# A row-wise gradient of an 8192 x 8192 matrix: the stores move from SyncE's DMA queue to ScalarE's

## The chip, the cores and the metric

The kernel runs on one core of one Trainium2 chip. A core has five engines with instruction streams of their own (TensorE, VectorE = DVE, ScalarE = ACT, GpSimd = POOL, SyncE = SP) and 16 DMA engines that move data between the chip's memory (HBM) and the core's on-chip memory (SBUF, 128 partitions). A DMA is issued by an instruction on one of the engines' streams; the instruction waits in that stream for its semaphores, and what it issues then joins that engine's DMA queue. The metric is the device time of one execution in microseconds (us), given as the median of several.

## The reference

The input is one float32 matrix, and the reference is one call:

```python
def setup_inputs():
    return {
        "x": np.random.randn(8192, 8192).astype(np.float32),
    }

def reference(x: np.ndarray) -> np.ndarray:
    return np.gradient(x, axis=1)
```

Along each row, every inner element becomes half the difference of its two neighbours, (x[j+1] - x[j-1]) / 2. The first element becomes x[1] - x[0], the last one x[8191] - x[8190]. Rows are independent. The kernel has to read 268.44 MB and to write 268.44 MB.

## The kernel before

The 8192 rows are cut into 32 sets of 256 rows. In a set, each of the 128 partitions holds two whole rows, 16384 numbers or 64 KB, side by side. A set is loaded with one DMA and stored with one DMA, each of 128 pieces of 64 KB (8.39 MB in all), so 8 pieces for each of the 16 DMA engines. The sets are grouped by three (`NB = 3`): in a group a partition's six rows are consecutive in memory, and set k of the group takes rows 2k and 2k+1 of the six. The last group has two sets.

There are three slots in SBUF, one for each set of a group, and set i lives in slot i % 3. A slot has 64 elements more than a set. The load puts the data behind that space (at `SH = 64`), and the result is written from the slot's beginning, so that the output overwrites input that has already been read. One slot therefore serves load, computation and store of a set in turn.

For each set, five steps follow each other:

- L55, the load, issued on SP's queue. A load of set i from 3 on needs the slot free, which is when the store of set i - 3 has landed.
- L65, POOL: the differences at the two ends of each row go into the small tile `ends` (128x4), before the computation overwrites them.
- L71, DVE: one custom instruction over the whole slot takes the differences of neighbours two apart and halves them (128x16382).
- L82, POOL for some sets and DVE for the others: the four end values are put in their places in the result.
- L84, the store of the set, which needs L82.

The order is written out by hand. SP's stream holds both kinds of DMA: the loads of sets 0, 1 and 2, then the stores of sets 0, 1 and 2, then the loads of sets 3, 4 and 5, then their stores, and so on to the end. The loop that produces this issues the store of set i on SP in each turn, and after the last set of a group it issues the loads of the whole next group. An instruction of SP's stream that waits holds up everything behind it in that stream. The helper `chain` declares which steps an instruction has to wait for: the load for the store of its slot, the first step for the load, and so on down to the store.

Of the kernel before, what the change touches and what calls it, by code (L numbers as in the profile page):

```python
# [1 line left out]

# [4 lines left out]


@with_exitstack
def kernel(  # L10
    ctx: ExitStack,
    tc: tile.TileContext,
    x: bass.AP,
    out: bass.AP,
):
    nc = tc.nc
    P = nc.NUM_PARTITIONS
    n, m = x.shape
    R = 2
    NB = 3  # L20
    SH = 64
    W = R * m
    nsets = n // (P * R)
    f32 = x.dtype

    def sets(a):
        found = []
        for first in range(0, nsets, NB):
            q = min(NB, nsets - first)
            rows = a[first * P * R : (first + q) * P * R, :].rearrange("(p q) m -> p (q m)", p=P)  # L30
            found += [rows[:, k * W : (k + 1) * W] for k in range(q)]
        return found

    x_sets, out_sets = sets(x), sets(out)

    pool = ctx.enter_context(tc.tile_pool(name="pool", bufs=1))
    pad = pool.tile([P, 32], f32, name="pad", tag="pad")
    slots = [pool.tile([P, SH + W], f32, name=f"slot{k}", tag=f"slot{k}") for k in range(NB)]
    ends = pool.tile([P, nsets, R, 2], f32, name="ends", tag="ends")
    loads, stores = [], [None] * nsets  # L40
    in_front = {}

    def chain(i, ins, *needed):
        group, engine = f"slot{i % NB}", ins.ins.engine
        keep = [o.ins for o in needed]
        if in_front.get(engine, (None,))[0] == group:
            keep.append(in_front[engine][1])
        tc.declare_no_dep(ins.ins, group=group, keep=keep, reason="implied by the needed step")
        tc.add_to_no_dep_group(group, ins.ins)
        in_front[engine] = group, ins.ins  # L50
        return ins

    def load(i):
        b = slots[i % NB]
        ins = nc.sync.dma_start(out=b[:, SH : SH + W], in_=x_sets[i])  # L55
        loads.append(chain(i, ins, *([stores[i - NB]] if i >= NB else [])))

    with tc.manual_schedule():
        for i in range(NB):
            load(i)  # L60
        for i in range(nsets):
            b = slots[i % NB]
            xin = b[:, SH : SH + W].rearrange("p (t m) -> p t m", m=m)

            ins = nc.gpsimd.tensor_sub(  # L65
                out=ends[:, i, :, :],
                in0=xin[:, :, 1 : m : m - 2],
                in1=xin[:, :, 0 : m - 1 : m - 2],
            )
            at = [chain(i, ins, loads[i])]  # L70
            ins = nc.vector._custom_dve(  # L71
                dve_ops.TENSOR_TENSOR_REDUCE_SUB_MAX,
                out=b[:, 1 : W - 1],
                in0=b[:, SH + 2 : SH + W],
                in1=b[:, SH : SH + W - 2],
                s0=0.0,
                s1=0.5,
            )
            halved = chain(i, ins, *at)
            res = b[:, 0:W].rearrange("p (t m) -> p t m", m=m)  # L80
            placer = nc.gpsimd if i % 5 in (1, 3) and i < nsets - 2 else nc.vector
            ins = placer.tensor_copy(out=res[:, :, 0 : m : m - 1], in_=ends[:, i, :, :])  # L82
            placed = chain(i, ins, halved)
            ins = nc.sync.dma_start(out=out_sets[i], in_=b[:, 0:W])  # L84
            stores[i] = chain(i, ins, placed)
            if i % NB == NB - 1:
                for k in range(i + 1, min(i + 1 + NB, nsets)):
                    load(k)


# [1 line left out]
_INS = ['x']  # L92
_OUTS = [((8192, 8192), 'float32')]


# [23 lines left out]
```

## Time and profile before

| | us |
|---|---|
| Median of 3 runs (1245.47 to 1245.9) | 1245.82 |
| Profiled execution | 1246.23 |
| Its span in the profile | 1244.3 |
| DVE busy, 52 instructions | 554.6 |
| of which L71, 32 instructions of 17.224 us | 551.2 |
| POOL busy, 48 instructions | 8.9 |
| Load, median from issue to landing | 57.9 |
| Store, median from issue to landing | 40.4 |

The profile is of one execution. Its span is a little shorter than the time measured for that execution. "Busy" counts the work of an engine's instructions; issuing a DMA and waiting for semaphores are not counted. The page cuts the span into 40 equal slices of 31.1 us, and gives for each the busy share of the engines and of the 16 DMA engines, with what they moved in GB/s. A row of the timeline gives the start, the duration, the engine (SPq is the instruction stream of SP as an issuer of DMAs), the line, the tiles and, in brackets, the idle time before it and what ended it. Several instructions of one kind in a row are drawn together as x3, and the duration is then from the first to the last of them. A row of the waits gives the total, the count and the longest. A row of the table by stretches gives the stretch, its length, the busy time of DVE and of POOL with counts, the granted clock, the DMA engines' busy share and GB/s. Beside these views the trace holds a record of each DMA packet, with its start, its duration and its size.

### The profile page before, as it was taken

To read this page: it belongs to the slowest core of one execution; us is meant where nothing else is said; L and a number is where in the kernel's file an instruction comes from. 1 tells how busy PE (TensorE), PEld (TensorE's weight loads), DVE (VectorE), ACT (ScalarE), POOL (GpSimd) and SP (SyncE) were. 2 spreads that over 40 slices of the span, in tenths; PEclk is the share of its full clock that TensorE was granted. 3 is DMA by queue.
4 is the path that set the end of the run, shared out by engine and by line. 5 is a ranking of instruction groups with operands and counts; after the bars stand their busy time and mean duration, and the time that the engine had idled before them with its cause. 6 is when DMAs were issued, how large, how long until landed. Compare 5 with 4: busy or idle time off the path is not lost.

```text
span 1244.3 us, 237 instructions
## 1 busy us (share of the span) xinstructions
DVE 554.6 (45%) x52; POOL 8.9 (1%) x48
## 2 busy tenths in 40 slices
DVE  2850583069009603850582079009603840591082
POOL 0000000000000000000000000000000000000000
DMA  9999999999999999999999999999999999999999
GB/s 404 438 436 423 421 438 438 438 438 436 434 423 430 434 438 438 430 436 432 428 434 436 432 436 434 438 436 430 432 428 438 436 434 438 434 434 430 430 409 404
DMA packets 9217, 536.88 MB, mean 431 GB/s; under 512 B 1024, under 2 KB 1024, under 8 KB 1024
## 3 DMA queue, kind: packets, MB, share of 16 engines
q1 hardware_dynamic: 9216, 536.88, 99.8%
q14 instruction: 1, 0.01, 0.0%
HBM read 268.44 MB, written 268.44 MB: 431 GB/s over the span
## 4 chain that ended last, share of the span: by engine, by line
another core or an unknown queue 74%; DVE 18%; DMA 3%; issue 2%; POOL 1%; SPq 0%; POOLq 0%
DVE slot L71 18%; DMA slot<-in_x_dram 3%; POOL ends L65 0%; POOL slot L82 0%; SPq L55 0%; POOLq L114 0%; DVE slot L82 0%
## 5 line engine op out<-in xcount | busy, mean ns | idle before, releaser
L71 DVE CUSTOM_DVE_ANT_0 slot<-slot 128x16382 f32<-128x16382 f32 x32 | 551.2, 17224 | 667.2 <-POOL ends L65 667.2
L65 POOL TENSOR_TENSOR ends<-slot 128x4 f32<-128x4 f32 x32 | 6.4, 200 | 988.1 <-DMA slot<-in_x_dram 988.1
L82 POOL COPY slot<-ends 128x4 f32<-128x4 f32 x12 | 2.3, 192 | 207.9 <-DVE slot L71 207.9
L82 DVE COPY slot<-ends 128x4 f32<-128x4 f32 x20 | 3.4, 172 | 0.7
L103 POOL MEMSET const-bfloat16-1.0<- 128x1 bf16 x1 | 0.1, 102 | 0.0
L103 POOL MEMSET const-uint8-127<- 128x1 uint8 x1 | 0.1, 102 | 0.0
L103 POOL MEMSET const-float32-0.0<- 128x1 f32 x1 | 0.1, 99 | 0.2 <-issue 0.2
L103 POOL MEMSET const-float32-1.0<- 128x1 f32 x1 | 0.1, 99 | 0.0
## 6 DMA issues: line engine op xcount, KB each, us to landing
slot<-in_x_dram SPq DMA_DIRECT2D x32, 57.9
out_dram<-slot SPq DMA_DIRECT2D x32, 40.4
```

What stands on the lines that cost most here:

```text
L65: ins = nc.gpsimd.tensor_sub(out=ends[:, i, :, :], in0=xin[:, :, 1 : m : m - 2], in1=xin[:, :, 0 : m - 1 : m - 2],)
L71: ins = nc.vector._custom_dve(dve_ops.TENSOR_TENSOR_REDUCE_SUB_MAX, out=b[:, 1 : W - 1], in0=b[:, SH + 2 : SH + W], in1=b[:, SH : SH + W - 2],
L82: ins = placer.tensor_copy(out=res[:, :, 0 : m : m - 1], in_=ends[:, i, :, :])
L103: nc = _bacc.Bacc("TRN2", target_bir_lowering=False, num_devices=1)
```

## The change

The store of each set is issued on ACT's stream and queue instead of SP's. SP's stream then holds the 32 loads alone, in the same order, and ACT's the 32 stores, in the same order; ACT has no other work. The load of set i from 3 on still waits for the store of set i - 3, and a store for the placed ends, but neither stands behind instructions of the other kind. Nothing changes on POOL or DVE.

```diff
@@ -81,7 +81,7 @@
             placer = nc.gpsimd if i % 5 in (1, 3) and i < nsets - 2 else nc.vector
             ins = placer.tensor_copy(out=res[:, :, 0 : m : m - 1], in_=ends[:, i, :, :])
             placed = chain(i, ins, halved)
-            ins = nc.sync.dma_start(out=out_sets[i], in_=b[:, 0:W])
+            ins = nc.scalar.dma_start(out=out_sets[i], in_=b[:, 0:W])
             stores[i] = chain(i, ins, placed)
             if i % NB == NB - 1:
                 for k in range(i + 1, min(i + 1 + NB, nsets)):
```

## The prediction

> **What bounds the kernel now.** I read the page from its top first: the span, the engines' rows, the slices, the queue's share.
>
> ```profile
> span 1244.3 us, 237 instructions
> ...
> DVE 554.6 (45%) x52; POOL 8.9 (1%) x48
> ...
> DMA  9999999999999999999999999999999999999999
> ...
> q1 hardware_dynamic: 9216, 536.88, 99.8%
> ```
>
> No engine is near the bound: DVE works 45% of the span. The 16 DMA engines are busy in all 40 slices, and the single queue q1 accounts for 99.8% of their time. What the transfers cost is the whole time.
>
> Next, how fast they run in each direction. The table by stretches takes stretches of 58 us, as long as a batch of three transfers:
>
> ```profile
> 2.00:60.00 58.00, 34.62 (x3) 0.59 (x3) 1.00 0.99 420
> 60.00:118.00 58.00, 17.39 (x2) 0.20 (x1) 1.00 1.00 434
> 118.00:176.00 58.00, 33.98 (x2) 0.59 (x3) 1.00 1.00 434
> 176.00:234.00 58.00, 18.03 (x4) 0.20 (x1) 1.00 1.00 434
> ```
>
> The last number is GB/s. The first and third rows are loads almost alone, the second and fourth stores almost alone: 434 GB/s both ways. The packet records behind these views say the same: a 64 KB packet takes 2.418 us in nearly every record and its engine starts the next one 2.415 us later, load or store. A transfer has 8 packets an engine, so 19.32 us. 64 transfers make 512 packets an engine: 512 x 2.415 = 1236.5 us of the 1244.3.
>
> Third, the order. The timeline at the start, and the waits of SP's queue:
>
> ```profile
> 0.74 1.33 SPq L55 DMA_DIRECT2D slot<-in_x_dram  x3
> ...
> 40.46 39.91 SPq L84 DMA_DIRECT2D out_dram<-slot  x3
> ...
> 81.69 39.18 SPq L55 DMA_DIRECT2D slot<-in_x_dram  x3
> ```
>
> ```profile
> SPq L84 <- DVE slot L82: 525.5, 20, 55.9
> SPq L55 <- DMA out_dram<-slot: 372.9, 29, 19.1
> SPq L84 <- POOL slot L82: 299.0, 12, 36.7
> ```
>
> SP stands waiting nearly always, and it costs nothing, because the transfers it has issued stand one behind the other: three loads, three stores, three loads. Store 0 is issued at 40.46 but its first packet starts at 61.4, behind loads 1 and 2. Load 3 is issued at 81.69, just after store 0 has landed, while stores 1 and 2 still have 38 us to run.
>
> Fourth, what is left over, from the packet records (means over 16 engines). 1.9 us to the first packet; 0.72 us extra on that packet; 1.02 us extra on the last load packet ahead of store 0, the first crossing from loading to storing; 0.95 us together on the last load packet at the nine later such crossings (0.19, 0.02, 0.12, 0.30, 0.12, 0.13, 0.03, 0.00, 0.04: mean 0.105); nothing of note at the ten crossings from stores to loads (0.02 at most); 1.7 us of empty DMA engines near the end, where store 30 is issued late; 1.4 us after the last packets. With 1236.5 that is 1244.2, the span. The end itself:
>
> ```profile
> 1203.28 19.61 SPq L84 DMA_DIRECT2D out_dram<-slot  x2
> 1204.86 0.20 POOL L65 TENSOR_TENSOR ends<-slot 128x4 f32<-128x4 f32 x1 [19.07 <-DMA slot<-in_x_dram]
> 1205.09 17.22 DVE L71 CUSTOM_DVE_ANT_0 slot<-slot 128x16382 f32<-128x16382 f32 x1 [1.84 <-POOL ends L65]
> 1222.35 0.17 DVE L82 COPY slot<-ends 128x4 f32<-128x4 f32 x1
> ```
>
> Load 31 ends, DVE takes 17.2 us, store 31 is issued about 1222.6 and its packets start at 1223.5; store 30 covers all but 1.7 us of that.
>
> **The change part by part.** The profiled execution took 1246.23 us, 1.93 beyond its span, and the median shown is 1245.82, 0.41 less. So I make the span's sum and add 1.5.
>
> *The issues themselves.* 32 store issues of about 0.34 us each (the row of L84) leave SP's queue and stand on ACT's. ACT has no work: the page has no row for it. An issue there waits, as before, for the placed ends (L82). Its semaphore waits on older transfers name ones that have landed before. Cost nothing: one issue against 38 us between stores, covered by whatever transfer is running. If that cover were gone, 32 x 0.34 = 11 us.
>
> *The wait that goes.* Load i+3 stood behind the issues of the whole batch of stores; now it waits only for store i. In the timeline what it ended on was the landing of store 0 anyway, and at that moment 38 us of stores were queued. Taking the wait away is worth 0 by itself: the DMA engines had no gap there to fill.
>
> *The wait that comes.* Stores no longer stand behind loads 1 and 2. Store 0's packets begin at about 40.5 + 0.9 = 41.4 us (0.9 is the time from issue to first packet of stores 30 and 31), while load 2's have just begun. From there two queues offer work to the same 16 engines. If they share evenly, a transfer takes 2 x 19.32 = 38.6 us instead of 19.3. Does a slot then starve the engines? A slot's round is load 38.6, about 18 of POOL and DVE (0.2 + 17.2 + 0.2 and the gaps), store 38.6, about 3 for issues and landings: 98 us. Three slots bring six transfers of work, 116 us. So 18 us are to spare: when a store lands, the next one has been ready for about 18 us. After each store's landing the load queue is empty for 1 to 3 us; the store queue has it all then, so the engines stay busy. Cost 0. It would turn into idle only if POOL and DVE took over 36 us a set.
>
> *The tail.* Loads and stores end in step, so load 31 is out when store 30 has most or all of its 8 packets left. Store 31 can start 21.0 us after load 31's mean end (1202.5 to 1223.5 in the rows), store 30 covers 19.3: the same 1.7 us gap, or 4.1 if one packet of store 30 (2.4 us) has already gone. I take 1.7.
>
> *The crossings.* This is the new work. Before, an engine crossed from loading to storing 11 times and back 10 times. Now the engine alternates. Load 2's 8 packets and the 232 of loads 3 to 31 each stand between store packets: about 240 crossings from load to store, and as many back. No stretch of this trace has both directions queued at once, so the price is bounded. Lower end: 0, by the crossings from store to load; below zero is a rival. Upper end: the first crossing, 1.02 us, x 240 = 245 us. It stands alone: the nine later crossings average 0.105 and the largest is 0.30. The slowest engine gives a nearer upper end: from the load issue at 81.69 to that at 1127.60 lie nine rounds of 116.21 us, 0.29 over 48 x 2.415 = 115.92. I take 0.105, the mean over engines of the steady crossings, since what is alternated is just such steady packets: 240 x 0.105 = 25.2 us. At 0.29 it is 69.6 us. The 1.97 us of old crossings go into this count.
>
> Sum: 1.9 + 0.7 + 1236.5 + 25.2 + 1.7 + 1.4 = 1267.4 us of span; with 1.5, **1269 us**.
>
> The Trainium skill (DMA: Bandwidth & Descriptors, Rules for kernel authors) states that spreading DMAs over SP, ACT and GpSimd does not raise bandwidth, as all run on the same 16 engines and interleave; by that the sum would stay without the 25.2 us, the first rival below. The same page (Latency and other measured facts) gives 214 GB/s in each direction as the full rate of copies on the two queues; as an estimate from that page, 536.88 MB at 428 GB/s is 1254 us, and with the ends 1261. No row here has both directions in flight, so the trace does not decide between them.
>
> **The rivals.**
>
> *Sharing is free.* The engines alternate at 2.415 us a packet. For it: the same rate in both directions and free crossings from store to load. Against: nine of ten times something was lost from load to store. 1.9 + 0.7 + 1236.5 + 1.7 + 1.4 + 1.5 = 1243.7 us, or 1246 with the longer tail.
>
> *The two directions overlap (the other side: faster).* One place: inside a DMA engine a load packet and a store packet run partly at once, from 41 us to 1202 us. Both kinds run at 434 GB/s alone, which fits a limit on each direction as well as a limit on the sum. A pair now takes 4.83 us; each 0.1 us less over 240 pairs is 24 us, so 1220. It decides from 0.002 us a pair on, since the free case lies just above the bound. Against: if the engine could take in the next packet's data while it puts out the last, the crossings from load to store should have been shortened, and they were lengthened.
>
> *Every crossing costs like the first, or in that direction.* Above 0.29 us each: beyond 1313 us, at 1.02 us 1489. For it: the first crossing is the only one into a fresh stream, and a second queue is one too. Against: nine later ones.
>
> **How the numbers follow.** About 0.2% (2.5 us) is what a measurement of this kernel can tell from no change: 1243.3 to 1248.3. Crossings at 0.02 to 0.29 us (1248.3 to 1313): 0.60. Free sharing: 0.20. Overlap: 0.11. Dear crossings: 0.09. Slower is 0.60 + 0.09 = 0.69, same 0.20, faster 0.11. The range from 1243 to 1314 leaves out the overlap and the dear crossings, 0.20.
>
> **What would show it.** Two queues in the page's third part, about half of the packets each. Loads and stores of 38 us to landing each, rather than 57.9 and 40.4. GB/s in the stretches from 60 us on: 425 by the forecast (434 x 4.83 / 4.94), 434 if sharing is free, above it if directions overlap. DVE's groups at 17.2 us and every store ready well ahead of its first packet; if the DMA row shows less than 9 in the middle, a slot starves and the 18 us were counted wrong. The packet records should be longer around alternations; if packets stand at 2.418 us and the time still grows, it is gaps between them. The prediction is wrong if the price of alternating isn't that of a crossing in one queue, which is its weakest step.

## The result, and the profile after

The changed kernel takes 1251.39 us in the median of five runs (1250.07 to 1255.29) against 1245.82 (1245.18 to 1245.94): a ratio of 1.0049, 95% interval 1.0034 to 1.0064. It is slower, as forecast, but by 5.6 us and not by 23. The runs also spread over 5 us, where those of the kernel before stay within 0.8. The profiled run, 1250.07 us, is the fastest of the five. Ratios, here and below, leave out the three runs that took over 1.5% more than the fastest of their kernel; the ranges hold them.

The page of the changed kernel, its span, DMA rows and queues:

```profile
span 1247.8 us, 264 instructions
...
DMA  9999999999999999999999999999999999999997
GB/s 403 437 437 437 437 424 426 429 435 435 437 437 437 437 437 437 435 426 424 429 437 435 435 437 435 437 437 437 437 429 426 433 431 437 433 437 437 437 437 311
...
q1 hardware_dynamic: 4608, 268.44, 49.8%
q10 hardware_dynamic: 4608, 268.44, 49.6%
```

The two queues halve the packets. The engines are full in every slice but the last: 311 GB/s there, where the kernel before had 404. The stretches, in the columns used before (length, DVE, POOL, clock, DMA share, GB/s):

```profile
60.00:118.00 58.00, 17.39 (x2) 0.20 (x1) 1.00 1.00 434
600.00:658.00 58.00, 24.32 (x3) 0.39 (x2) 1.00 1.00 434
1000.00:1058.00 58.00, 20.80 (x2) 0.59 (x3) 1.00 1.00 434
1208.00:1227.00 19.00, 17.39 (x2) 0.20 (x1) 1.00 0.65 283
1227.00:1247.00 20.00, 0.00 (x0) 0.00 (x0) 1.00 0.97 419
```

With loads and stores sharing the engines the rate is 434 GB/s, the very number of pure loading and pure storing. The loss is in the fourth row: for 19 us the engines are 65% busy. The timeline of that place:

```profile
1208.62 0.20 POOL L65 TENSOR_TENSOR ends<-slot 128x4 f32<-128x4 f32 x1 [38.31 <-DMA slot<-in_x_dram]
1208.85 17.22 DVE L71 CUSTOM_DVE_ANT_0 slot<-slot 128x16382 f32<-128x16382 f32 x1 [21.07 <-POOL ends L65]
1226.11 0.17 DVE L82 COPY slot<-ends 128x4 f32<-128x4 f32 x1
```

POOL sees load 31 at 1208.62 (1204.86 before). DVE works until 1226.3, store 31 follows, and the engines have run out of store 30 by then: 6.1 us of empty engines in the mean, by the packet records, against 1.7 before.

The packet records show how the queues share: from store 0's first packet on, wherever both queues have work, an engine takes one whole 64 KB packet of the one and then one of the other, each 2.418 us long. Between 100 and 1190 us 87% of the packets follow one of the other queue. The Trainium skill (DMA: Bandwidth & Descriptors, Queues, rings and completion order) states that an engine goes round-robin over its queues and switches at packet boundaries only; the records agree, packet by packet. The Trainium skill's rule that two issuing engines only interleave (same page, Rules for kernel authors) was the better of the two weighed ahead: 434 GB/s is above 428, the estimate from the 214 GB/s in each direction that the Trainium skill (same page, Latency and other measured facts) states for copies between HBM tensors.

For what follows, two quantities from the packet records. The *lateness* of an engine is how far its packets are behind 1.75 us + 2.415 us a packet; the slowest of the 16 counts, because a transfer has landed only when all have done their part. (The records don't name the engine. They are put in 16 chains by their times; in each chain every transfer has 8 packets and one record of 4 bytes behind them.) The *landing delay* is the time from the last packet of a load to POOL's start on it. In this trace the delay is 0.41 and 0.37 us for loads 0 and 1, which ran alone, and 2.82 to 3.17 from load 2 on, which shared: 2.4 us more, the length of one packet of the other queue. The 4-byte records say why. For loads 0 and 1 this record starts as soon as the engine's last packet has ended. On the engine that finishes last with load 31 it starts at 1208.21, one store packet (2.41 us) after the load's last packet, and POOL starts 0.41 us later; it is the same 2.41 us for every load from 2 on. What reports a landing waits its turn, too.

The first account of the 3.5 us between the profiled spans: load 31's last packet ends at 1205.8, where it was 1204.5 (+1.3: the slowest engine is 6.2 us late and no longer 4.9); POOL starts on it 2.82 us later and not 0.35 (+2.5); from POOL's start to the end it is 39.2 us and was 39.4 (-0.2).

### The profile page after: what moved, and what is told of

Same layout as the page of the kernel before. It is cut to its first block, busy times and chain, and to the rows that moved or that the text cites. A ratio compares the mean times of both kernels' runs of the same rounds, so it can differ in the third digit from the quotient of the medians.

```text
span 1247.8 us, 264 instructions
## 1 busy us (share of the span) xinstructions
DVE 554.6 (44%) x52; POOL 8.8 (1%) x48
## 4 chain that ended last, share of the span: by engine, by line
another core or an unknown queue 83%; DMA 9%; issue 3%; DVE 3%; SPq 1%; POOL 0%; POOLq 0%
DMA slot<-in_x_dram 5%; DMA out_dram<-slot 3%; DVE slot L71 3%; SPq L55 1%; POOL ends L65 0%; DVE slot L82 0%; POOLq L114 0%
```

## The experiments

**Is it the end or the sharing?** Four kernels. First, the last two stores back on SP's queue:

```diff
-            ins = nc.scalar.dma_start(out=out_sets[i], in_=b[:, 0:W])
+            storer = nc.sync if i >= nsets - 2 else nc.scalar
+            ins = storer.dma_start(out=out_sets[i], in_=b[:, 0:W])
```

> Stores 30 and 31 go back to SP's queue, where they stand behind load 31; stores 0 to 29 stay on ACT's. Theory 'tail' (alternating packets is free; the loss is the 6.1 us, mean over DMA engines, in which they stand empty ahead of store 31, because part of store 30 has already gone beside load 31): store 30 lies whole behind load 31 again, the gap is about 1.7 us as before the change, and the time is 1245 to 1247 us. Theory 'mixing' (sharing the engines costs a little all the way from 41 us on): the time stays at 1250 to 1252 us.

Measured: 1251.43 us (1248.03 to 1255.31), ratio 1.0044 (1.0028 to 1.0060). 'Tail' as I had put it missed; the time is that of 'mixing'. Second, only the last eight stores on ACT's queue:

```diff
-            ins = nc.scalar.dma_start(out=out_sets[i], in_=b[:, 0:W])
+            storer = nc.scalar if i >= nsets - 8 else nc.sync
+            ins = storer.dma_start(out=out_sets[i], in_=b[:, 0:W])
```

> Only stores 24 to 31 are issued on ACT's queue, stores 0 to 23 stay on SP's. 'Tail': the end is that of the changed kernel, so nearly the whole loss is there, 1249 to 1252 us, with 4 to 7 us of empty engines ahead of store 31. 'Mixing': the two directions share the engines for a quarter of the sets, so a quarter of the 5.6 us of loss, 1247.2 us.

Measured: 1256.9 us (1255.37 to 1258.14), ratio 1.0083: a quarter of the sharing costs more than all of it. That speaks against a price for each shared packet ('mixing' had 1247.2), and is beyond what 'tail' allowed. The ends of these two:

```profile
1213.85 0.20 POOL L65 TENSOR_TENSOR ends<-slot 128x4 f32<-128x4 f32 x1 [35.68 <-DMA slot<-in_x_dram]
1214.09 17.23 DVE L71 CUSTOM_DVE_ANT_0 slot<-slot 128x16382 f32<-128x16382 f32 x1 [18.45 <-POOL ends L65]
```

```profile
1217.02 0.20 POOL L65 TENSOR_TENSOR ends<-slot 128x4 f32<-128x4 f32 x1 [39.07 <-DMA slot<-in_x_dram]
1217.25 17.22 DVE L71 CUSTOM_DVE_ANT_0 slot<-slot 128x16382 f32<-128x16382 f32 x1 [21.84 <-POOL ends L65]
```

The first is that with the last two stores on SP, the second that with the last eight on ACT. Load 31 is seen 9 and 12 us later than in the kernel before, and their spans, 1253.3 and 1256.2, are again 39.4 and 39.2 us after that. The packet records say why it is late: in each trace one engine has fallen far behind, 13.9 and 14.6 us by the end of load 31, while the mean engine is 3.6 and 4.5 behind at 1150 us. Of the 13.9 us, 11.9 are lost on load packets followed by a store, some 0.3 us at a time; of the 14.6, 9.5, and 4.3 more on store packets followed by a load, where the sharing begins. The first of the two also shows the landing report by itself: at its end ACT's queue is empty beside load 31, the 4-byte record follows the last packet at once, and POOL starts 0.37 us after that packet.

Third and fourth, the last set computed and stored row by row, in the changed kernel and in the kernel before (there with `nc.sync`):

```diff
+            if i == nsets - 1:
+                res = b[:, 0:W].rearrange("p (t m) -> p t m", m=m)
+                for r in range(R):
+                    ins = nc.vector._custom_dve(
+                        dve_ops.TENSOR_TENSOR_REDUCE_SUB_MAX,
+                        out=b[:, r * m + 1 : (r + 1) * m - 1],
...
+                    ins = nc.scalar.dma_start(
+                        out=out_sets[i][:, r * m : (r + 1) * m], in_=b[:, r * m : (r + 1) * m]
+                    )
+                    stores[i] = chain(i, ins, placed)
+                continue
```

> The changed kernel, but the last set (31) is computed and stored row by row: two halves of 8.6 us on DVE, two stores of half the size. 'Tail': the first half store is ready about 8.6 us earlier than store 31 was, ahead of the end of store 30, so the gap of 6.1 us closes: 1244.5 to 1246 us, and the spread from run to run shrinks to under 1 us. 'Mixing': no work is taken away before that, 1250 to 1252 us.

> The same split of the last set in the kernel before, all DMAs on SP's queue. Both theories: the 1.7 us gap ahead of store 31 closes and nothing else changes, 1244.1 us (1243.7 to 1244.8). Against the split with stores on ACT's queue it tells whether anything of the change's cost is left outside the tail: 'tail' puts the two within 1.5 us of each other, 'mixing' 4 to 6 us apart.

Measured: 1252.62 us (1249.5 to 1256.76) and 1246.36 us (1245.63 to 1246.85, ratio 1.0002, 0.9993 to 1.0010). Both expectations missed (the first is just above the 1250 to 1252 of 'mixing'). In the kernel before, the 1.7 us gap stayed, because it lies ahead of store 30 and not of store 31: my reading of the tail had it at the wrong store. It costs nothing there either, since the slowest engine (4.9 us late) has no gap at all. In the changed kernel the split does close the gap (0.7 us are left of 6.1), but the slowest engine, 7.9 us late in this trace, never stood empty, and now it alone ends the kernel: an engine without lateness would end the span at about 1239.5 us (1.75 + 512 x 2.415, and 1.2 after the last packet), and 1239.5 + 7.9 is the 1247.4 of this span.

**A laggard.** So I formed another theory: alternating is free for most engines; a few fall out of step with the others, lose time at their crossings from load to store, and the slowest one sets the end. Four runs on it. The changed kernel once more:

> The changed kernel again, for one more trace. New theory, 'laggard': alternating costs most DMA engines nothing, but one engine or a few fall out of step with the others, and pay some 0.3 us at a few dozen of their crossings from load to store; the slowest engine's lateness (its time beyond 2.415 us a packet from 1.75 us on) was 6.2 us in the trace of the changed kernel, 11.3 with the last two stores on SP's queue, 13.3 with only the last eight on ACT's, 4.9 in the kernel before. Load 31 lands when its slowest engine has finished, and everything after that hangs on it. So the profiled time should be 1244 plus the slowest engine's lateness, within 1 us. Rival, 'tail alone': the time varies with how many packets of store 30 have gone ahead, and not with the lateness.

Measured: 1252.02 us; its slowest engine is 8.3 us late, so 1252.3 was expected. Of the latenesses in that expectation two are too low: by the records they are 13.9 and 14.6 us, not 11.3 and 13.3. With 14.6 the rule gives 1258.6 for the last eight stores on ACT (1258.14 was measured). With 13.9 it gives 1257.9 for the last two on SP, 2.6 above the 1255.31 of the profiled run: that is the turn that the landing report didn't have to wait there. Then one queue, but with loads and stores in turn:

```diff
-            if i % NB == NB - 1:
-                for k in range(i + 1, min(i + 1 + NB, nsets)):
-                    load(k)
+            if i >= 1 and i + 2 < nsets:
+                load(i + 2)
```

> The kernel before, one queue, but its order is load, store, load, store from store 1 on, and no longer three and three: 31 crossings from load to store where there were 11, none of them between two queues. If every crossing costs the mean engine 0.105 us and the slowest 0.29, as the prediction had it, the slowest engine loses 20 x 0.29 = 5.8 us more: 1250 to 1252 us. If a crossing is only dear after a long stretch of one direction, 1245 to 1246.5 us. The gap of 1.7 us ahead of store 30 closes in either case, since a load lies between.

Measured: 1246.95 us (1245.98 to 1247.67), ratio 1.0004 (0.9995 to 1.0013), slowest engine 4.7 us late; the gap of 1.7 us hasn't closed, it now lies ahead of store 31 (1.6 us). Nearly three times the crossings in one queue cost nothing: the price is not one of crossings as such. Next, POOL's and DVE's work left out (the input is stored as it came), with two queues and with one:

```diff
...
-            ins = nc.scalar.dma_start(out=out_sets[i], in_=b[:, 0:W])
-            stores[i] = chain(i, ins, placed)
+            ins = nc.scalar.dma_start(out=out_sets[i], in_=b[:, SH : SH + W])
+            stores[i] = chain(i, ins, loads[i])
```

> All work of POOL and DVE is left out: the input is stored as it came, stores on ACT's queue. No chain of 38 us behind load 31 any more, so the end is that of the slowest DMA engine alone. 'Laggard': slowest engine 6 to 11 us late, 1245.5 to 1251 us, and 1 to 6 us above the same with one queue; the spread from run to run stays at some us. 'Tail alone': no more than 1.5 us above the same with one queue.

> The same without POOL's and DVE's work with all DMAs on SP's queue, three loads and three stores in turn: slowest engine about 4.9 us late, the gap of 1.7 us gone, 1244.5 to 1246 us by both theories.

Measured: 1260.48 us (1254.6 to 1260.92) and 1246.51 us (1245.88 to 1248.09). With one queue it is 0.5 us above the expected range, with the slowest engine 4.8 us late. With two it is 14 us above that, far over the 1 to 6 expected: sharing alone, without any chain behind load 31, costs more here than in the changed kernel. Its stretches (no DVE column, as DVE does nothing):

```profile
60.00:118.00 58.00, 0.00 (x0) 1.00 1.01 434
600.00:658.00 58.00, 0.00 (x0) 1.00 1.00 429
1000.00:1058.00 58.00, 0.00 (x0) 1.00 1.00 429
```

The engines are full throughout and yet move 429 GB/s: here packets themselves are longer. By the records five engines are 18 us late at 1150 us and the mean one 11.9. The slowest ends 19.0 us late, and 1239.5 + 19.0 is the span, 1258.4, within 0.1 us.

How the crossings from load to store fared in the records of shared packets between 100 and 1190 us, and how often the engines were out of step (between 4 and 12 of the 16 on a store packet):

```
kernel                          out of step  mean loss   over 50 ns
changed, first trace               16%          2.5 ns      0.9%
changed, after_look1               50%          9.3 ns      3.1%
last two stores on SP              21%         11.3 ns      3.6%
last eight on ACT (from 960 us)    44%         34.5 ns     11.1%
no POOL and DVE work, two queues   71%         50.9 ns     13.4%
```

Most crossings are free, and those over 50 ns cost 0.27 to 0.38 us in the mean. One engine has many of them: 15 of the 28 in the first trace, 34 of the 99 with the last two stores on SP. But that it is being out of step that makes a crossing dear is not shown, and the records speak against it: taken at the middle of the load packet, 2.7% of the crossings out of step cost over 50 ns in after_look1 and 3.7% of those in step, and without POOL's and DVE's work 13.0% and 13.9%; of the 28 in the first trace 21 were in step.

**The end, and where the stores join.** Three runs. The last three stores on SP, behind loads 30 and 31:

```diff
+            last = i >= nsets - 3
+            if i % NB == NB - 1 and last:
+                for k in range(i + 1, nsets):
+                    load(k)
-            ins = nc.scalar.dma_start(out=out_sets[i], in_=b[:, 0:W])
+            storer = nc.sync if last else nc.scalar
+            ins = storer.dma_start(out=out_sets[i], in_=b[:, 0:W])
...
-            if i % NB == NB - 1:
+            if i % NB == NB - 1 and not last:
```

> The changed kernel, but stores 29, 30 and 31 go on SP's queue, and loads 30 and 31 are issued ahead of all three. Load 31 then ends with 58 us of stores behind it, and nothing on the other queue beside it. Theory: the change's cost has two parts, the lateness of the slowest DMA engine (6 to 8 us against 4.9) and, at the end, the landing of load 31, which is seen 2.8 us after its last packet where it was 0.35, since the count-up at its end waits its turn behind a packet of the other queue; all later work hangs on it. This takes the second part away: load 31 seen 0.3 to 0.5 us after its last packet, no empty engines before the end other than by lateness, a profiled time of 1241.5 plus the slowest engine's lateness, and a median of 1248 to 1250 us, about 2.5 below the changed kernel. If the landing were not on the path, the median stays at 1251 to 1252.

Measured: 1251.21 us (1246.64 to 1269.6), ratio 1.0038 (1.0021 to 1.0056). The time settles nothing, for a reason of my making: load 31 waits for store 28 with nothing behind it, and in the trace the engines stand empty for 9.5 us between 1163 and 1176 us. The landing delay did fall, to 0.36 us for load 30 and 0.42 for load 31. The kernel with the last two stores on SP holds the case that was meant: by this expectation's rule its profiled time is 1241.5 + 13.9 = 1255.4 us, and it took 1255.31. Next, DVE's work cut to the first row of two:

```diff
-                out=b[:, 1 : W - 1],
-                in0=b[:, SH + 2 : SH + W],
-                in1=b[:, SH : SH + W - 2],
+                out=b[:, 1 : m - 1],
+                in0=b[:, SH + 2 : SH + m],
+                in1=b[:, SH : SH + m - 2],
```

> The changed kernel with DVE's work cut to the first of a partition's two rows: 8.7 us a set, the differences of the second row are left out. Store 0 is issued 8.6 us earlier, so it joins in the middle of load 1 and not at the start of load 2. Without any work of POOL and DVE the engines stood out of step (between 4 and 12 of the 16 storing) 71% of the time and the time was 9 us more than with it. If the moment at which the stores join sets how far engines fall out of step, this kernel lies between: 1252 to 1260 us, with more crossings from load to store that cost over 50 ns than the 0.9% of the changed kernel. If not, the chain behind load 31 is 8.6 us shorter and the time is that of the slowest engine alone, 1246 to 1250 us.

Measured: 1261.22 us (1259.93 to 1262.67), ratio 1.0121 (1.0108 to 1.0134). Less work made it 10 us slower, just above the 1252 to 1260 of the first case. 7.4% of the crossings cost over 50 ns, but the engines are out of step only 20% of the time, so that share does not order the kernels by itself. One engine is 21.3 us late at 1150 us, where the next is 7.6; it has 42 of the 179 dear crossings, and from then on it never stands empty. It alone ends the kernel: 1239.5 + 21.3 = 1260.8, and the span is 1260.7. Both kernels in which store 0 joins during load 1 (here after six of its eight packets, without POOL and DVE work after two) are dear, which fits the moment of joining; in the changed kernel it joins after two packets of load 2. I haven't varied that moment alone. The changed kernel again:

> The changed kernel once more. By the two parts: profiled time 1244 us plus the slowest engine's lateness, within 1 us (6.2 gave 1250.07, 8.3 gave 1252.02), and every load after the second seen 2.8 to 3.2 us after its last packet. If the lateness is not what sets the spread from run to run, it misses by more than 1 us.

Measured: 1259.7 us. The slowest engine is 16.1 us late, so 1260.1 was expected, and every load after the second is seen 2.8 to 3.2 us after its last packet: both as expected. The end, as stretches:

```profile
1218.00:1222.00 4.00, 3.19 (x1) 0.20 (x1) 1.00 0.80 344
1222.00:1237.00 15.00, 14.20 (x2) 0.00 (x0) 1.00 0.05 22
1237.00:1257.00 20.00, 0.00 (x0) 0.00 (x0) 1.00 0.97 419
```

For 15 us the engines are 5% busy: they wait for DVE, and DVE for load 31, whose last packet ends at 1215.7. It is the 496th of its engine, and 1.75 + 496 x 2.415 + 16.1 is that time. One engine does all this: the mean engine was through with load 31 at 1203.3, and 37 of the 97 dear crossings are the slowest one's. The 5% are that engine, alone at work on store 30.

**More samples, and the addresses.** The changed kernel and the one with the split last set beside each other, and a changed kernel whose output rows are moved by 13 sets:

```diff
-            ins = nc.scalar.dma_start(out=out_sets[i], in_=b[:, 0:W])
+            ins = nc.scalar.dma_start(out=out_sets[(i + 13) % nsets], in_=b[:, 0:W])
```

> The changed kernel, for more samples: 1250 to 1256 us, a spread of some 5 us or more, the profiled span equal to the time of load 31's last packet plus 2.8 us of landing, 18.6 us to the first packet of store 31, 19.4 us of packets and 1.2 us, within 0.5 us.

> The changed kernel with the last set computed and stored by halves, once more. If the wait for load 31's landing is a part of its own, the median is 2 to 4 us below that of the changed kernel beside it, and the profiled span is 1239.5 us plus the slowest engine's lateness. If the lateness alone decides, the two medians agree within their spread.

> The changed kernel, but set i's result goes to the rows of set i + 13 (in a ring of 32), so that the store's addresses stand otherwise against the load's; the output's rows are permuted by that. If the addresses bring the slow crossings, the share of crossings over 50 ns leaves the 1 to 4% of the changed kernel, and the time leaves 1250 to 1256 us, in one of the two directions. If they come from engines that store while others load, wherever the rows lie, both stay.

Measured: 1252.54 us (1248.11 to 1263.52, ratio 1.0069, 1.0042 to 1.0096), 1254.05 us (1244.78 to 1265.42, ratio 1.0056, 1.0035 to 1.0078) and 1253.0 us (1247.82 to 1259.92, ratio 1.0057, 1.0038 to 1.0075). The changed kernel's span, 1248.4 us, is within 0.1 of the expected sum, load 31's last packet ending at 1206.3. The moved rows change nothing in the times, which speaks against the relative place of the addresses as the cause; one other place was tried. In the profiled run of that kernel 0.4% of crossings cost over 50 ns and the slowest engine is 3.3 us late, below the changed kernel's traces; its run, at 1247.82 us, was one of the two fastest of the twelve. The split kernel's trace fits its formula (span 1245.5, lateness 6.0, 1239.5 + 6.0):

```profile
1208.00:1227.00 19.00, 17.62 (x4) 0.20 (x1) 1.00 1.00 433
1227.00:1240.00 13.00, 0.00 (x0) 0.00 (x0) 1.00 0.95 408
```

The gap before the last store is closed: 433 GB/s where the changed kernel had 283. But the median does not fall, against my expectation of 2 to 4 us. With runs from 1245 to 1265, a part of that size can't be seen in medians, or the lateness eats it.

The traces with the full chain behind load 31:

```
kernel                    POOL starts on load 31   span     between   slowest engine late   landing delay
before                          1204.86           1244.3     39.4          4.9                 0.4
changed, first trace            1208.62           1247.8     39.2          6.2                 2.8
changed, after_look1            1210.89           1250.1     39.2          8.3                 2.8
changed, after_look2            1218.58           1257.8     39.2         16.1                 2.9
changed, after_more             1209.17           1248.4     39.2          6.5                 2.8
last two stores on SP           1213.85           1253.3     39.4         13.9                 0.4
last eight stores on ACT        1217.02           1256.2     39.2         14.6                 2.8
output rows moved               1206.70           1245.9     39.2          3.3                 2.9
one queue, load and store in turn  1204.62        1244.1     39.4          4.7                 0.4
```

The column "between" is what settles it: the profiled time is the moment at which load 31 is seen, plus a constant. That moment is 1199.6 us (1.75 + 496 x 2.415) plus the last two columns, within 0.25 us in all rows but one. With the moved rows it is 0.9 us later, since there an engine that is only 1.8 us late, but has one packet of store 30 ahead of load 31's last, comes last.

## Why the prediction was right and wrong

**What bounds the kernel, the rates, the issues:** right. 434 GB/s in the shared stretches, DVE's instruction at 17.22 us, no empty engines in the middle, and no cost of the issues on ACT. Loads and stores were forecast at 38 us to landing; the page has longer times, since they count waiting behind the transfer before:

```profile
slot<-in_x_dram SPq DMA_DIRECT2D x32, 43.6
out_dram<-slot ACTq DMA_DIRECT2D x32, 54.6
```

**The wait that comes:** right in that no slot starves. Store 0's first packets start at 46.7 to 47.3 us, though, after two packets of load 2, and not at 41.4: the 0.9 us from issue to first packet were read where all transfers stood in one queue.

**The crossings:** this is the term that failed. I took 0.105 us for each of 240 crossings, 25.2 us. In the first trace the mean crossing costs 2.5 ns, in the second 9.3, and an engine has 210 of them: 0.5 to 2.0 us in all. The row I took the price from is one in which all engines turn from a batch of 24 loads to stores; one queue with 31 crossings showed that not even that price goes with their number. And I charged the mean engine, where the end is set by the slowest. Its lateness is the cost: 6.2, 6.5, 8.3 and 16.1 us in the four traces of the changed kernel against 4.9, different each time, which is also the spread. So the forecast had the right place, load packets ahead of a store, with a price far too high for most engines, and it had no part for the few that fall behind. That 1251.39 us lies between 1248.3 and 1313, the interval given to crossings of 0.02 to 0.29 us, is luck: the mean crossing costs less than 0.02, and the kernel is slower by two parts that the sum didn't have, the slowest engine and the landing report.

**The tail:** sized wrongly, at 1.7 us with 4.1 as its worst, and the 1.7 was read at the wrong store. Of the 6.1 us of the first trace 3.8 come from load 31 being seen late: 2.5 us of landing delay, which no row of the kernel before could show since nothing shared its queue, and 1.3 us of the slowest engine.

**The rivals:** 'sharing is free' is true of the rate, and with its longer tail (1246 us) came as near to 1251.39 as any sum; what it lacked is the landing delay and the laggard. 'Overlap' is excluded by 434 GB/s. 'Dear crossings' exist, at 0.3 us in the mean, but for 1 to 4% of the crossings in the traces of the changed kernel.

What stays open: why one engine pays so often at its crossings and falls behind, whether it is the same engine each time, and whether the moment at which the stores join matters. No version here beats the kernel before: one queue with loads and stores in turn is level with it at 1.0004.

## What to carry to other kernels

When transfers are the bound and one queue keeps the DMA engines full, a second queue has no rate to give; look at what the end hangs on, and count the landing of the last load by its slowest engine and by what shares that engine. A mean over 16 engines prices the rate, not the landing. A price read where all engines change direction together should not be multiplied by the number of changes in another pattern.

## What the runs showed of the hardware that I had not expected

Two queues alternate in whole 64 KB packets at no loss of rate (434 GB/s; 429 with POOL's and DVE's work left out). A load that shares its engines is seen 2.8 to 3.2 us after its last packet, since the 4-byte record that reports it waits 2.41 us for a packet of the other queue, and 0.36 to 0.42 when alone. With two queues a single engine can fall 3 to 21 us behind in 1200 us while the mean is 2 to 6 behind (12 with POOL's and DVE's work left out), and halving DVE's work made the kernel 10 us slower, by one such engine.
